# Linear half of six groups of up tiles per layer by Strassen's scheme for three of four k pairs; gating on GpSimd, scaled tokens from the third group on

## The chip, the core and the metric

The kernel runs on one core of a Trainium2 chip. Its engines are TensorE (PE in the profile; PEld is its weight load), VectorE (DVE), ScalarE (ACT), GpSimd (POOL) and SyncE (SP), which issues most DMAs. The metric is device time in microseconds (us) of one execution, taken as the median of several runs.

## The reference

A trunk of two layers over 512 tokens of width 1024, in fp32. Each layer mixes tokens (differential attention in layer 0, chunked gated linear attention in layer 1, cross-attention into a memory in both), projects the result, and then runs a gated MLP with a causal depthwise convolution of width 3. The change lies in that MLP alone:

```python
def rms_norm(x, g):
    return x * lax.rsqrt(jnp.mean(x * x, axis=-1, keepdims=True) + EPS) * g

def conv_ffn(h, w_up, conv_w, conv_b, w_down):
    u = h @ w_up                                   # (512, 1024) @ (1024, 5632)
    c = causal_depthwise_conv3(u, conv_w) + conv_b
    a, g = jnp.split(c, 2, axis=-1)                # linear half, gate half: 2816 each
    return (jax.nn.silu(g) * a) @ w_down           # (512, 2816) @ (2816, 1024)

for i in range(2):
    ...
    h = rms_norm(x, ffn_norm[i])
    x = x + conv_ffn(h, w_up[i], conv_w[i], conv_b[i], w_down[i])
```

## The kernel before

Everything is kept transposed: a tile has 128 features on the partitions and the 512 tokens along the free axis. An fp32 product is made of three fp32r products: both operands are split into a high part (a cast, on ACT) and a low part (the difference, on DVE), and the terms high·high, high·low and low·high are summed in PSUM. `product` (L387 to L389) issues these three for each k tile of 128.

**Weights** come in an order fixed by a plan of pieces, packed by the host into blocks of up to 1024 columns. A block is loaded raw by SP (three buffers), and `split_weights` makes `whi` (ACT, L255) and `wlo` (DVE, L258) of it; there are six buffers of each (`WB`). A k tile of an up piece has 256 columns, so a block holds four k tiles and a piece two blocks.

**The feed-forward** of a layer (`ffn`) runs 11 groups, numbered 0 to 10, in three parts (`HALVES` = 4, 4, 3). A group has two output tiles of the linear half (piece `ua`) and two of the gate half (piece `ug`), taken in turn: linear 0, gate 0, linear 1, gate 1. Each output tile has one PSUM bank and eight k tiles, 24 matmuls of 512 columns. The eight banks have the tags mm, sm, lg and tp, two of each, and go round in the order `TURNS`. The operands are the tokens' high and low halves `xsh`, `xsl` as they are before the norm's row scale; `row_scales` computes that scale, rB, during group 0, and each output tile is multiplied by it afterwards. Behind a tile's last matmul follow, in `conv`: the product with rB (DVE, in place in PSUM, L1165), the last tap with scale and bias (ACT, L1167) and the other two taps (DVE, L1168 and L1169). A gate tile then gets silu (ACT, L1333), the gating product with its linear tile is done on DVE (L1334), and the result, `mid`, is split into high (ACT, L1190) and low (DVE, L1191). The results of convolutions rotate through six buffers, `cvo`.

**A down stage** follows each part and multiplies its `mid` tiles by `w_down`. Two k tiles of one piece form a 2x2 block problem (two k tiles by two output tiles, tokens in a left and a right half of 256), which is done by Strassen's scheme in Winograd's form: seven products of 256 columns in place of eight (`seven`, L1247), with sums of weights, sums of operands and a decode of sums at the end. Sums of operands are made in `combine` (L1198 to L1201, four operations of 256 columns into a tile `tsum`, on POOL, or on DVE for the last group of a part); sums of weights in `combined` (L287 to L290, four operations on POOL into one of two tiles `wsum`), which are then split like other weights (ACT L291 and L294, DVE L292 and L295). The decode is L1258 to L1266. Four pieces in the last part of layer 0 and one in that of layer 1 are done whole, by eight products.

The order of instructions on each engine is the program's own order as written, adjusted by the scheduler of the framework; `order` rows below show it. An engine works its list in order, so an instruction that waits holds back all behind it.

Of the kernel before, what the change touches and what calls it, by code (L numbers as in the profile page):

```python
# [32 lines left out]
WB = 6  # L33
# [52 lines left out]
def _pieces():  # L86
# [6 lines left out]
    for l in range(2):  # L93
# [45 lines left out]

TURNS = ('mm', 'mm', 'sm', 'sm', 'lg', 'lg', 'tp', 'tp')  # L140
# [42 lines left out]
def trunk(ctx, tc, head_d, x_t, mem_t, wpack, cols_a_d, cols_d, conv_d, gate_d, rel_bias, diff_lambda, consts, onehot, out):  # L183
# [94 lines left out]
    def combined(raw, n):  # L278
# [4 lines left out]
        r, wsum = full(raw), sum_pool[0].tile([128, WTILE], F32, name="wsum", bufs=2)  # L283
        a12, a22, a11, a21 = (r[:, :, i] for i in range(4))
        sv = wsum[:, :512 * pairs].rearrange("p (i j c) -> p i j c", i=4, j=pairs)
        s1, s2, s3, s4 = (sv[:, i] for i in range(4))
        ADD.tensor_add(s1, a21, a22)  # L287
        ADD.tensor_sub(s3, a11, a21)
        ADD.tensor_sub(s2, s1, a11)
        ADD.tensor_sub(s4, a12, s2)  # L290
# [3 lines left out]
        A.copy(h1[:, m], wsum[:, m])  # L294
        V.tensor_sub(l1[:, m], wsum[:, m], h1[:, m].bitcast(F32))  # L295
        out = []
        for j in range(pairs):
            own = lambda t, i: t[:, 512 * j + 128 * i:512 * j + 128 * i + 128]
            new = lambda t, i: t[:, 128 * (pairs * i + j):128 * (pairs * i + j) + 128]
# [3 lines left out]
        return out  # L303

    def make_block(raws=None):
# [9 lines left out]
        if plan[i][0][0] == "dn":  # L315
            made[i] += combined(raw, n)
# [8 lines left out]
    ADD = G  # L325


    def weights(key, by_block=False):
# [3 lines left out]
        if i + 1 < len(plan) and plan[i + 1][0][0] in ("dn", "dw"):  # L332
            limit = first_of[i + 1] + 1
# [814 lines left out]
    def ffn(pool, l, acc):  # L1148
        rB = pool.tile([128, S], F32, name="rB", bufs=1)
        sum_pool[0] = pool  # L1150
        old = list(zip(xh, xl))
        nu = [0]
# [4 lines left out]
        def up(parts, n, ops):  # L1157
            i = nu[0]
            nu[0] += 1
            p = bank(TURNS[i % 8])  # L1160
            product(p, parts, n, ops)
            return p

        def conv(p, j):
            V.tensor_mul(p, p, rB)  # L1165
# [27 lines left out]
        left, right = blk(0, 256), blk(1, 256)  # L1193

        def combine(b2, b1, bh, bl, fh, fl, E):
            t = pool.tile([128, 2 * S], F32, name="tsum", bufs=1)
# [15 lines left out]
        def down(base, nq, mids, pairs, tags, last, acc2):  # L1212
# [88 lines left out]
            if whole[3]:  # L1301
                start(3)
                while done[0] < first_of[first + 4]:
                    make_block()
# [139 lines left out]
```

## Time and profile before

| | |
|---|---|
| median of 3 runs | 1149.63 us (1149.5 to 1149.68) |
| the profiled execution, its own time | 1150.36 us |
| its span, first to last instruction | 1148.5 us |
| feed-forward of layer 0 | some 240 to 594 us of the span; its down stages at 328 to 368 and 456 to 496 |
| feed-forward of layer 1 | some 792 to 1136 us; its down stages at 880 to 920, 1007 to 1048 and 1113 to 1136 |

A row of a group gives the line, the engine, the operation with output and input tile (partitions x elements and type), the number of instructions, and after the bar the total busy time, the mean duration of one in ns, and the idle time of the engine just before them with what ended it. A row of a timeline gives the start, the duration, the engine and the instruction, and in brackets how long the engine waited for what before it. A row of windows gives a stretch of the span, its length, the busy time of each engine with its count of instructions, the granted TensorE clock (1.00 is full speed), the DMA share and GB/s. A matmul's record overlaps with the next one's, so the pace is read from a window, not from the duration of one.

### The profile page before, as it was taken

The page shows a single profiled execution, that of the slowest core. Times are in us where ns is not written, and L with a number is a line of the kernel's source. Part 1 is how long each engine was busy: PE and PEld are TensorE (multiplying, and loading weights), DVE is VectorE, ACT ScalarE, POOL GpSimd, SP SyncE. Part 2 cuts the span into 40 slices and gives each one's busy share as a digit, 9 for nine tenths or more (in the row PEclk, how much of TensorE's full clock was granted, in tenths as well). Part 3 has the DMA queues.
Part 4 walks back from the last instruction along what each step waited for, and adds up shares of the span by engine and source line. Part 5 has one row for each costly group of instructions (what it writes and reads, how often), then busy time and mean ns, then how long its engine had stood idle before and what let it go on. Part 6 is the DMA issues. An engine that isn't in the chain of part 4 may idle for free.

```text
span 1148.5 us, 16655 instructions
## 1 busy us (share of the span) xinstructions
PE 1142.7 (99%) x6311; PEld 985.1 (86%) x6311; DVE 871.2 (76%) x1455; ACT 592.0 (52%) x1032; POOL 193.2 (17%) x230
## 2 busy tenths in 40 slices
PE   9999999999999999999999999999999999999998
PEld 7888888888899888988888888988888988899887
DVE  8576778688789677977677637777887977797777
ACT  6676686555454354434457634535644444453442
POOL 0000000001543125500000000000135403360340
PEclk9999999999999999999999999999999999999999
DMA  9522242133214322343252220333241342234212
GB/s 293 173 83 84 78 142 74 58 109 110 92 57 146 111 77 80 96 144 100 69 182 70 100 94 12 101 125 119 74 126 40 127 149 74 61 91 143 92 46 102
DMA packets 39662, 117.83 MB, mean 103 GB/s; under 512 B 4767, under 2 KB 7256, under 8 KB 39582
## 3 DMA queue, kind: packets, MB, share of 16 engines
q1 hardware_dynamic: 39150, 116.37, 31.8%
q8 instruction: 50, 0.82, 0.3%
q10 hardware_dynamic: 432, 0.39, 0.1%
q14 instruction: 30, 0.25, 0.1%
HBM read 112.54 MB, written 4.21 MB: 102 GB/s over the span
## 4 chain that ended last, share of the span: by engine, by line
PE 99%; DMA 0%; DVE 0%; ACT 0%; issue 0%
PE ps_mm L365 6%; PE ps_mm L367 6%; PE ps_mm L366 6%; PE ps_mm L387 6%; PE ps_mm L388 6%; PE ps_mm L389 6%; PE ps_lg L1247 5%; PE ps_sm L388 5%; PE ps_sm L389 5%; PE ps_sm L387 5%; PE ps_mm L1247 4%; PE ps_tp L388 4%; PE ps_lg L388 4%; PE ps_tp L387 4%; PE ps_lg L387 4%; PE ps_tp L389 4%
## 5 line engine op out<-in xcount | busy, mean ns | idle before, releaser
L258 DVE TENSOR_TENSOR wlo<-raw,whi 128x1024 fp32r<-128x1024 f32 (+4 forms) x174 | 194.2, 1127 | 77.0 <-ACT whi L255 76.4
L255 ACT CAST whi<-raw 128x1024 fp32r<-128x1024 f32 (+4 forms) x174 | 168.0, 976 | 124.2 <-PE ps_sm L388 29.8
L365 PE MATMUL ps_mm<-whi,xsh 128*128 128x512 f32 (+2 forms) x328 | 126.2, 385 | 0.0
L367 PE MATMUL ps_mm<-whi,xsl 128*128 128x512 f32 (+2 forms) x328 | 123.0, 375 | 0.0
L366 PE MATMUL ps_mm<-wlo,xsh 128*128 128x512 f32 (+2 forms) x328 | 122.8, 374 | 0.0
L387 PE MATMUL ps_mm<-xsh,whi 128*128 128x512 f32 x278 | 109.3, 393 | 0.0
L388 PE MATMUL ps_mm<-xsl,whi 128*128 128x512 f32 x278 | 108.4, 390 | 0.0
L389 PE MATMUL ps_mm<-xsh,wlo 128*128 128x512 f32 x278 | 108.2, 389 | 0.0
L387 PE MATMUL ps_sm<-xsh,whi 128*128 128x512 f32 x218 | 84.8, 389 | 0.0
L388 PE MATMUL ps_sm<-xsl,whi 128*128 128x512 f32 x218 | 84.8, 389 | 0.0
L389 PE MATMUL ps_sm<-xsh,wlo 128*128 128x512 f32 x218 | 84.8, 389 | 0.0
L365 PEld LDWEIGHTS ps_mm<-whi,xsh 128*128 128x128 f32 x328 | 61.7, 188 | 11.4 <-issue 1.0
L367 PEld LDWEIGHTS ps_mm<-whi,xsl 128*128 128x128 f32 x328 | 61.7, 188 | 11.3
L366 PEld LDWEIGHTS ps_mm<-wlo,xsh 128*128 128x128 f32 x328 | 61.8, 188 | 10.1
L387 PE MATMUL ps_lg<-xsh,whi 128*128 128x512 f32 x160 | 62.2, 389 | 0.0
L388 PE MATMUL ps_lg<-xsl,whi 128*128 128x512 f32 x160 | 62.2, 389 | 0.0
L389 PE MATMUL ps_lg<-xsh,wlo 128*128 128x512 f32 x160 | 62.2, 389 | 0.0
L387 PE MATMUL ps_tp<-xsh,whi 128*128 128x512 f32 x160 | 62.2, 389 | 0.0
L388 PE MATMUL ps_tp<-xsl,whi 128*128 128x512 f32 x160 | 62.2, 389 | 0.0
L389 PE MATMUL ps_tp<-xsh,wlo 128*128 128x512 f32 x160 | 62.2, 389 | 0.0
L389 PEld LDWEIGHTS ps_mm<-xsh,wlo 128*128 128x128 f32 x278 | 52.2, 188 | 11.0
L387 PEld LDWEIGHTS ps_mm<-xsh,whi 128*128 128x128 f32 x278 | 52.2, 188 | 10.8 <-issue 0.3
(382 smaller groups left out, 2835.4 us busy)
## 6 DMA issues: line engine op xcount, KB each, us to landing
raw<-in_wpack_dram SPq DMA_DIRECT2D x178, 512.0 KB, 3.5
xt<-in_x_t_dram SPq DMA_DIRECT2D x15, 256.0 KB, 5.2
raw<-in_wpack_dram SPq DMA_DIRECT2D x15, 256.0 KB, 3.1
raw<-in_wpack_dram SPq DMA_DIRECT2D x8, 384.0 KB, 3.0
xres<-xt SPq DMA_DIRECT2D x8, 256.0 KB, 3.2
xt<-xres SPq DMA_DIRECT2D x8, 256.0 KB, 5.8
out_dram<-xt SPq DMA_DIRECT2D x7, 256.0 KB, 2.0
bt<-bias_d SPq DMA_DIRECT2D x6, 256.0 KB, 4.1
```

Of the source, the lines that this page charges most:

```text
L255: ins = A.copy(hi[:, c], raw[:, c])
L258: V.tensor_sub(lo[:, c], raw[:, c], hi[:, c].bitcast(F32))
L365: mm(p, sh[k][:, blk(b)], hi, start=k == 0, stop=False)
L366: mm(p, sh[k][:, blk(b)], lo, start=False, stop=False)
L367: mm(p, sl[k][:, blk(b)], hi, start=False, stop=k == KT - 1)
L387: mm(p, hi[:, blk(n)], bh, start=i == first, stop=False)
L388: mm(p, hi[:, blk(n)], bl, start=False, stop=False)
L389: mm(p, lo[:, blk(n)], bh, start=False, stop=i == last)
L1247: mm(banks[c][b][:, h], w, v, start=b not in seen[c], stop=m == nq - 1 and t == 2 and i in close)
```

## The change

Six groups of each layer, 4 to 9 (`SEVEN`), compute the linear half by seven products where they can. The piece `ua` of such a group takes its k tiles in the order (6,7), (4,5), (0,1), (2,3). The pair (6,7) is done by eight products as before; the other three pairs by seven products of 256 columns, summed over the pairs in four banks and decoded once (`up_by_seven`). So both linear tiles of such a group come before its gate tiles. `combined` gets a count of plain pairs: the first block of a piece keeps one pair plain and makes sums for one pair, the second makes sums for two.

The scheme needs sums of tokens in which a row scale cannot be taken out behind, since the decode adds up products. From group 2 on (`SCALED`) the operands are therefore tokens already multiplied by rB: `scaled` multiplies on POOL (L1294), scales by the norm's gain on ACT (L1295), and `scaled_token` splits them (L1265, L1266): tokens 0 to 2 behind the second tile pair of group 0, 3 to 5 behind the first of group 1, 6 and 7 behind the second of group 1. `conv` leaves the rB product out from group 2 on. `token_sums` scales two tokens again and makes their sums on POOL, once a layer: for (4,5) behind the second tile pair of group 2, for (0,1) and (2,3) behind the two of group 3.

The gating product goes to POOL (L1428), but for the last group of each part, where it stays on DVE. Sums of weights, of `mid` tiles and of tokens now share the two tiles `wsum`; `mid2` has 8 buffers instead of 9. Weight blocks are made by one `refill` in up and down stages, within the six buffers, and banks come from a running counter over `TURNS`. The bytes and the number of loads stay as they were.

```diff
-                piece(("ua", l, q), "w_up", l, K8, (256 * q, 256 * q + 256))
+                ks = (6, 7, 4, 5, 0, 1, 2, 3) if q in SEVEN else K8
+                piece(("ua", l, q), "w_up", l, ks, (256 * q, 256 * q + 256))
...
+SCALED = 2
+SEVEN = (4, 5, 6, 7, 8, 9)
...
-    def combined(raw, n):
+    def combined(raw, n, plain):
...
-        r, wsum = full(raw), sum_pool[0].tile([128, WTILE], F32, name="wsum", bufs=2)
-        a12, a22, a11, a21 = (r[:, :, i] for i in range(4))
+        r, wsum, js = full(raw), sum_tile(), pairs - plain
+        a12, a22, a11, a21 = (r[:, plain:, i] for i in range(4))
...
-        A.copy(full(h0)[:, :, :3], r[:, :, :3])
-        V.tensor_sub(full(l0)[:, :, :3], r[:, :, :3], full(h0)[:, :, :3].bitcast(F32))
-        m = slice(0, 512 * pairs)
+        if plain:
+            c = slice(0, 512 * plain + 384)
+            split_weights(c, raw, h0, l0)
+        else:
+            A.copy(full(h0)[:, :, :3], r[:, :, :3])
+            V.tensor_sub(full(l0)[:, :, :3], r[:, :, :3], full(h0)[:, :, :3].bitcast(F32))
+        m = slice(0, 512 * js)
...
+    def sum_tile():
+        return sum_pool[0].tile([128, WTILE], F32, name="wsum", bufs=2)
...
+        def take(n):
+            nb[0] += n
+            return [bank(TURNS[i % 8]) for i in range(nb[0] - n, nb[0])]
+
+        def refill():
+            nonlocal live
+            while done[0] < min(len(order), first_of[min(used[0] + 2, len(plan))]) and live + sizes[done[0]] <= WB:
+                live += sizes[done[0]]
+                make_block()
...
+        def up_by_seven(i):
+            b, seen = take(4), set()
+            where = [(2, left), (0, left), (0, right), (1, left), (3, right), (2, right), (3, left)]
+            for m, ks in enumerate(((6, 7), (4, 5), (0, 1), (2, 3))):
+                while len(made) <= i or len(made[i]) <= m:
+                    refill()
+                part = made[i][m]
+                if m == 0:
+                    for n in range(2):
+                        product(b[n], part, n, [tokens[k] for k in ks], range(2), 99)
+                else:
+                    for r in steps:
+                        c, h = where[r]
+                        (hi, lo), (vh, vl) = part[r], sums_of[ks][r]
+                        for t, (w, v) in enumerate(((hi, vh), (hi, vl), (lo, vh))):
+                            mm(b[c][:, h], w, v, start=c > 1 and c not in seen, stop=m == 3 and t == 2 and r in (2, 5, 6, 3))
+                            seen.add(c)
+                if m % 2:
+                    release(i, 2, m == 3)
+            u, w = ctile(), ctile()
+            A.copy(u[:, left], b[2][:, left])
+            V.tensor_add(w[:, right], u[:, left], b[2][:, right])
+            V.tensor_add(u[:, right], w[:, right], b[3][:, right])
+            V.tensor_add(w[:, left], w[:, right], b[3][:, left])
+            V.tensor_add(w[:, right], u[:, right], b[3][:, left])
+            V.tensor_add(b[0], b[0], u)
+            V.tensor_add(b[1], b[1], w)
+            return b[:2]
 
-        def conv(p, j):
-            V.tensor_mul(p, p, rB)
+        def conv(p, j, scaled):
+            if not scaled:
+                V.tensor_mul(p, p, rB)
...
-            t = pool.tile([128, 2 * S], F32, name="tsum", bufs=1)
+            t = sum_tile()
...
+        def scaled(k):
+            t = ctile()
+            G.tensor_mul(t, xT[k], rB)
+            A.activation(t, t, AF.Copy, scale=c_ffn(l, k))
+            return t
+
+        def scaled_token(k):
+            t = scaled(k)
+            if k < 6:
+                y = pool.tile([128, 2 * S], F32R, name="hsc", bufs=6)
+                hi, lo = y[:, :S], y[:, S:]
+            else:
+                hi, lo = split_tiles()
+            parts_of(t, hi, lo)
+            return hi, lo
+
+        def token_sums(ks):
+            (bh, bl), (fh, fl) = (tokens[k] for k in ks)
+            tiles = [split_tiles() for _ in range(2)]
...
+            combine(scaled(ks[0]), scaled(ks[1]), None, None, None, None, G, parts)
...
+                if q == SCALED:
+                    tokens = fresh
+                a, c2, ops, ca = begin(("ua", l, q)), [], [], None
+                if q in SEVEN:
+                    ca = [conv(p, 2 * q + n, True) for n, p in enumerate(up_by_seven(a))]
...
-                    V.tensor_mul(ca, ca, cg)
-                    c2.append(ca)
+                    end = q == base + nq - 1
+                    (V if end else G).tensor_mul(cn, cn, cg)
+                    c2.append(cn)
...
+                    if 0 < 2 * q + n < 4:
+                        fresh += [scaled_token(k) for k in range(len(fresh), min(len(fresh) + 3, KT))]
+                    if SEVEN and 4 < 2 * q + n < 8:
+                        token_sums(((4, 5), (0, 1), (2, 3))[2 * q + n - 5])
```

In the rows below `[waits ...]` names the engines and DMA queues whose earlier work an instruction waits for. The first place is ACT at the end of group 1 in layer 0, where `cvo`, `mid` and `xsh` are the tiles of that name above. Before:

```order
L255 CAST whi<-raw 128x1024 [waits DMAHW0_49,PE_49]
L1190 CAST mid<-cvo 128x512 [waits DVE_49]
L1167 ACTIVATE cvo<-ps_tp,cv_81 128x512 [waits DVE_49]
L255 CAST whi<-raw 128x1024 [waits DMAHW1_49,PE_49]
L255 CAST whi<-raw 128x1024 [waits DMAHW2_49,PE_49]
L1167 ACTIVATE cvo<-ps_tp,cv_81 128x512 [waits DVE_49]
L1333 ACTIVATE cvo<-cvo 128x512 [waits DVE_49,Activation_49]
L1190 CAST mid<-cvo 128x256 [waits DVE_49]
L1190 CAST mid_3002<-tsum 128x1024 [waits Pool_49]
```

The same place now:

```order
L1242 ACTIVATE cvo<-ps_tp,cv_81 128x512 [waits DVE_49]
L258 CAST whi<-raw 128x1024 [waits DMAHW1_49,PE_49]
L1242 ACTIVATE cvo<-ps_tp,cv_81 128x512 [waits DVE_49]
L1295 ACTIVATE cvo<-cvo,cols 128x512 [waits Pool_49] x2
L258 CAST whi<-raw 128x1024 [waits DMAHW2_49,PE_49]
L1426 ACTIVATE cvo<-cvo 128x512 [waits DVE_49,Activation_49]
L1265 CAST mid<-cvo 128x256 [waits Pool_49]
L1265 CAST xsh<-cvo 128x512 [waits Activation_49] x2
L1265 CAST mid_3059<-wsum 128x1024 [waits Pool_49]
```

Two scalings of tokens (6 and 7) have come between the convolution (L1242, before L1167) and silu (L1426, before L1333), and the casts of these two tokens stand behind the cast of `mid`, which now waits for POOL's gating.

The second place is POOL where the sums of weights for the first down stage of layer 0 are made. Before, sums of `mid` tiles and of weights stand beside each other:

```order
L1198 TENSOR_TENSOR tsum<-cvo 128x256 [waits DVE_49]
L1200 TENSOR_TENSOR tsum<-cvo 128x256
L1199 TENSOR_TENSOR tsum<-cvo,tsum 128x256 [waits Pool_49]
L1201 TENSOR_TENSOR tsum<-cvo,tsum 128x256 [waits Pool_49]
L287 TENSOR_TENSOR wsum<-raw 128x256 [waits DMAHW0_49,DVE_49]
L288 TENSOR_TENSOR wsum<-raw 128x256
L289 TENSOR_TENSOR wsum<-wsum,raw 128x256 [waits Pool_49]
L290 TENSOR_TENSOR wsum<-raw,wsum 128x256 [waits Pool_49]
```

Now the token scalings and token sums stand between the sums of weights (L290 to L293 are before's L287 to L290):

```order
L290 TENSOR_TENSOR wsum<-raw 128x256 [waits DMAHW7_49,DVE_49]
L291 TENSOR_TENSOR wsum<-raw 128x256
L292 TENSOR_TENSOR wsum<-wsum,raw 128x256 [waits Pool_49]
L293 TENSOR_TENSOR wsum<-raw,wsum 128x256 [waits Pool_49]
L1294 TENSOR_TENSOR cvo<-xt,rB 128x512 x2
L1271 TENSOR_TENSOR wsum<-cvo 128x256 [waits DVE_49,Activation_49]
L1273 TENSOR_TENSOR wsum<-cvo 128x256
L1272 TENSOR_TENSOR wsum<-cvo,wsum 128x256 [waits Pool_49]
L1274 TENSOR_TENSOR wsum<-cvo,wsum 128x256 [waits Pool_49]
L290 TENSOR_TENSOR wsum<-raw 128x256 [waits DMAHW0_49,DVE_49]
L291 TENSOR_TENSOR wsum<-raw 128x256
L292 TENSOR_TENSOR wsum<-wsum,raw 128x256 [waits Pool_49]
```

The sums of tokens go into `wsum`, wait for ACT's scaling, and the next block's sums stand behind them in the list.

The third place is ACT at the border between the groups 6 and 7 of layer 0, ahead of the second down stage; this is the list as it is now, whose L1229 is the copy that opens the decode of a linear half:

```order
L1265 CAST mid<-cvo 128x512 [waits Pool_49]
L258 CAST whi<-raw 128x1024 [waits DMAHW4_49,PE_49]
L1242 ACTIVATE cvo<-ps_mm,cv_81 128x512 [waits PE_49]
L1426 ACTIVATE cvo<-cvo 128x512 [waits DVE_49,Activation_49]
L298 CAST whi<-raw 128x2x384 [waits DMAHW5_49,PE_49]
L1265 CAST mid<-cvo 128x256 [waits Pool_49]
L1265 CAST mid_4616<-wsum 128x1024 [waits Pool_49]
L301 CAST whi<-wsum 128x1024 [waits PE_49,Pool_49]
L1229 COPY cvo<-ps_lg 128x256 [waits PE_49]
L298 CAST whi<-raw 128x2x384 [waits DMAHW6_49,PE_49]
L301 CAST whi<-wsum 128x1024 [waits PE_49,Pool_49]
```

The decode's copy stands behind the cast of `mid` and the cast of its sums, both of which wait for POOL, and behind a cast of sums of weights.

More of the change, by code (lines that the diff above doesn't have):

```diff
@@ L1235, in release, with emitted, seven @@
-            def release(c, m):
-                nonlocal live
-                piece = first + c
+            def start(c):
+                begin(("dw" if whole[c] else "dn", l, base, c))
+                banks[c] = take(2 if whole[c] else 4)
+            def emitted(c, m):
                 if m == nq - 1 or m % 2:
-                    live -= 1 if whole[c] else 2
+                    release(first + c, 1 if whole[c] else 2, m == nq - 1)
+            def seven(c, m, some=steps):
+                while len(made) <= first + c or len(made[first + c]) <= m:
@@ L1240, in release @@
                     refill()
-            def seven(c, m, some=steps):
                 for i in some:
@@ L1354, in ffn @@
                     load(gw[32 * b:32 * b + 17], gate_d)
-            down(base, nq, mids, pairs, nu[0] // 4 % 2, last, acc2)
+            down(base, nq, mids, pairs, last, acc2)
             base += nq
```

148 lines of the change are left out of this document (79 added, 69 removed).

## The prediction

> **What bounds the kernel now.** Groups are numbered 0 to 10 as in the program; down stages follow groups 3, 7 and 10. I read the page first: busy shares, then the chain that ended last.
>
> ```profile
> PE 1142.7 (99%) x6311; PEld 985.1 (86%) x6311; DVE 871.2 (76%) x1455; ACT 592.0 (52%) x1032; POOL 193.2 (17%) x230
> PE 99%; DMA 0%; DVE 0%; ACT 0%; issue 0%
> ```
>
> TensorE is the whole chain; nothing else ever ends a wait. So an edit gains what it takes from PE's stream, and loses whenever another engine becomes late for PE. For the price of a matmul I took windows of PE alone, one inside an up stage (512 columns), one inside a down stage (256 columns, already by seven products):
>
> ```profile
> core 0: us, PE busy (x), PEclk, DMA share, GB/s
> 260.00:320.00 60.00, 60.00 (x266) 1.00 0.29 94
> 330.00:366.00 36.00, 36.00 (x303) 1.00 0.35 111
> ```
>
> Without the two or three that only reach over an edge: 60/264 = 0.227 us for 512 columns, 36/300 = 0.120 us for 256. The half width costs 0.53 of the full one. Next, how much room the other engines have, from windows of all engines: the first two groups of the feed-forward, then the first two down stages of layer 0.
>
> ```profile
> core 0: us, PE busy (x) PEld busy (x) DVE busy (x) ACT busy (x) POOL busy (x), PEclk, DMA share, GB/s
> 255.90:289.30 33.40, 33.40 (x149) 27.67 (x148) 29.69 (x39) 18.51 (x23) 3.06 (x4) 1.00 0.35 111
> 328.00:368.00 40.00, 40.00 (x334) 39.96 (x333) 37.91 (x52) 19.07 (x25) 22.10 (x20) 1.00 0.36 110
> 456.00:496.00 40.00, 40.00 (x335) 40.00 (x334) 37.23 (x50) 18.56 (x25) 18.25 (x19) 1.00 0.36 115
> ```
>
> DVE's average of 76% hides that it is 89 to 95% busy exactly here. PE has no wait in these stretches, but no reserve behind it.
>
> **The gain.** One pair of k tiles costs 12 matmuls of 512 (2.73 us) by eight products, 21 of 256 (2.52 us) by seven: 0.21 us less. Six groups, three pairs, two layers are 36 pairs: **7.4 us**, and that is all that PE can gain. If the cover of the rest holds, the run ends at 1150.4 - 7.4 = 1143.0 (the profiled execution took 1150.36; the median of the runs is 0.7 less).
>
> **The work around it**, from groups of instructions with shapes apart:
>
> ```profile
> L290 POOL TENSOR_TENSOR wsum<-raw,wsum 128x256 f32<-128x256 f32 x35 | 42.7, 1221 | 2.7
> L289 POOL TENSOR_TENSOR wsum<-wsum,raw 128x256 f32<-128x256 f32 x35 | 37.4, 1068 | 0.0
> L288 POOL TENSOR_TENSOR wsum<-raw 128x256 f32<-128x256 f32 x35 | 30.9, 882 | 0.0
> L1201 POOL TENSOR_TENSOR tsum<-cvo,tsum 128x256 f32<-128x256 f32 x14 | 10.3, 737 | 0.7
> L288 POOL TENSOR_TENSOR wsum<-raw 128x128 f32<-128x128 f32 x3 | 1.4, 462 | 0.0
> L258 DVE TENSOR_TENSOR wlo<-raw,whi 128x1024 fp32r<-128x1024 f32 x143 | 172.7, 1219 | 70.7 <-ACT whi L255 70.2
> L295 DVE TENSOR_TENSOR wlo<-wsum,whi 128x1024 fp32r<-128x1024 f32 x35 | 47.9, 1368 | 1.5 <-ACT whi L294 1.3
> L1334 DVE TENSOR_TENSOR cvo<-cvo 128x512 f32<-128x512 f32 x44 | 33.3, 757 | 15.9 <-ACT cvo L1333 15.9
> L1165 DVE TENSOR_TENSOR ps_sm<-ps_sm,rB 128x512 f32<-128x512 f32 x24 | 16.6, 693 | 1.4 <-PE ps_sm L389 1.3
> L1191 DVE TENSOR_TENSOR mid<-cvo,mid 128x512 fp32r<-128x512 f32 x28 | 19.7, 704 | 2.4 <-ACT mid L1190 2.1
> L1261 DVE TENSOR_TENSOR cvo<-cvo,ps_lg 128x256 f32<-128x256 f32 x10 | 4.2, 421 | 0.8
> L294 ACT CAST whi<-wsum 128x1024 fp32r<-128x1024 f32 x35 | 36.7, 1049 | 25.3 <-POOL wsum L290 14.5 <-PE ps_sm L388 7.3 <-PE ps_tp L388 3.5
> L1190 ACT CAST mid<-cvo 128x512 fp32r<-128x512 f32 x28 | 17.3, 619 | 8.8 <-DVE cvo L1334 8.0
> L345 ACT ACTIVATE xsh<-xt,cols 128x512 fp32r<-128x512 f32 x16 | 11.5, 716 | 3.9 <-DVE xt L1111 3.9
> ```
>
> DVE loses 72 scalings by rB (x 0.693 = 50 us) and 32 gatings (x 0.757 = 24). It gains twelve decodes of four 256-column and two 512-column sums (4 x 0.421 + 2 x 0.69 = 3.1, 37 us), the low halves of 1152 more weight columns a piece (sums included: 3200 where there were 2048; 12 x 1.37 x 1152/1024 = 18), 16 scaled tokens and 12 halves of token sums (28 x 0.704 = 20). 74 against 75: even. POOL gains 180 instructions: 96 weight sums, 24 token sums, 32 gatings and 28 token scalings. The last 60 have 512 columns, which the trace does not show on POOL: 256 against 128 columns differ by 0.275 (0.737 - 0.462, the quickest rows), so 0.737 + 2 x 0.275 = 1.29 us alone.
>
> POOL's price depends on DVE. In the timeline:
>
> ```profile
> 331.18 1.21 DVE L295 TENSOR_TENSOR wlo<-wsum,whi 128x1024 fp32r<-128x1024 f32 x1
> 331.33 1.66 POOL L290 TENSOR_TENSOR wsum<-raw,wsum 128x256 f32<-128x256 f32 x1
> 333.08 0.75 DVE L1169 SCALAR_TENSOR_TENSOR cvo<-ps_tp,cv,cvo 128x510 f32<-128x510 f32 x1
> 333.66 0.73 POOL L288 TENSOR_TENSOR wsum<-raw 128x256 f32<-128x256 f32 x1
> ```
>
> Under a DVE subtraction with both inputs in SBUF, 256 columns take 1.66 us; beside one that reads PSUM, 0.73. The four weight sums average about 1.01. So 512 columns in company: 1.29 x 1.01/0.737 = 1.77.
>
> [...]
>
> **Place A, start of group 2.** It is the first to use scaled tokens, and PE reaches tokens 6 and 7 with its 19th product. Timeline of before at that border (PE starts group 2 at 284.67):
>
> ```profile
> 284.67 0.39 PE L387 MATMUL ps_mm<-xsh,whi 128*128 128x512 f32 x1
> 288.75 0.39 PE L387 MATMUL ps_mm<-xsh,whi 128*128 128x512 f32 x1
> 286.79 0.78 ACT L1167 ACTIVATE cvo<-ps_tp,cv 128x512 f32<-128x512 f32 x1 [1.09 <-DVE ps_tp L1165]
> 289.41 0.63 ACT L1333 ACTIVATE cvo<-cvo 128x512 f32<-128x512 f32 x1 [1.85 <-DVE cvo L1169]
> 290.07 0.69 DVE L1334 TENSOR_TENSOR cvo<-cvo 128x512 f32<-128x512 f32 x1 [0.76 <-ACT cvo L1333]
> 290.80 0.41 ACT L1190 CAST mid<-cvo 128x256 fp32r<-128x256 f32 x1 [0.76 <-DVE cvo L1334]
> ```
>
> ACT's new order puts the casts of tokens 6 and 7 behind that last cast, which waits for POOL's gating, which waits for silu. Before, the cast ends at 291.21. Now two scalings (2 x 0.716) and a weight cast (1.05) stand between convolution and silu, 0.6 beyond the 1.85 it waited anyway; gating takes 1.29 for 0.69, 0.6 more; token 6's cast adds 0.62: 293.0 against 288.75, and its low half (0.70 against a matmul's 0.23) 0.5 more: 4.7 us. DVE was 29.69 of 33.40 busy ahead of it; six low halves (4.2) less three gatings (2.3), and POOL in company, make it about 3.5 later, and gating in company 0.5. **8.7 us; layer 1 has one weight cast more before the convolution, 9.7.** Bounds 4.7 and 12 each.
>
> **Place B, first down stage.** From the end of group 2 to the last weight sum of this stage POOL's list holds 44 operations of 256 columns and five of 512, where before it held 24. It cannot begin before silu, 5.4 us in, that is 16.4 before the stage. In company: 44 x 1.01 + 5 x 1.77 = 53.3, done at +36.9. That block is needed at +35.3 (fourth piece, third product group: 14 x 2.52), less cast and low half (1.05 + 1.37): +32.9. 4.0 late, if POOL never waits. It does: token sums wait for ACT's scaling, and weight sums now share two buffers with token and end-group sums that DVE must first read (ACT and DVE each twice round, about 4 x 2 us). DVE, 37.91 of 40 full, cannot catch up. **12 us per layer**; alone (0.737, 1.29) POOL is done at +22.5 and only the buffer wait is left, 2.5; at 1.22 per operation 20.
>
> **Place C, groups 4 to 7 and the second down stage.** After a group's last matmul (0): weight cast 1.05 and convolution to 2.0, DVE's low half and two steps to 3.9, silu 4.5, gating 6.3, cast 6.7, five POOL operations 11.8, cast 12.8; three narrow sums meanwhile, cast and copy to 14.2. But the next linear half is done at 10.3, so its decode is 3.9 late; with it and two weight halves 19.7, convolutions 23.0. The gate half's first tile, its silu, gating and casts follow in order, and the next last convolution starts at 28.6, where 22.5 would be on time: **6.1 us lag per group** (3.5 by the prices alone). After two borders 12.2; the down stage takes the banks of group 7's linear half 21.9 after the border, while its convolutions end at 23 + 12.2 + 1.5 = 36.7: 14.8 (7.2 alone), part of it perhaps already at group 7's own banks. The stage's late last sums add 2: **17 us per layer**. The third stage in layer 1 has only two such groups and a plain one behind: 2 in all.
>
> **Sum:** 18.4 + 24 + 34 + 2 - 7.4 = +71; 1150.4 + 71 - 0.7 = **1221 us**. DMAs, attention and the tail keep their counts: nothing.
>
> **Rivals.** (1) *The saving arrives*, PE never waits: 1142. For it: DVE's total is even and every engine's average has room. It decides if POOL's sums and gating run so early that no list holds PE's operands back; the lists above put them behind silu. (2) *Only latency, no contention*: POOL at 0.74 and 1.29. A 14, B 5, C 18: 1150.4 + 37 - 7.4 = 1180. For it: DVE's PSUM operations do not disturb POOL. Against: weight sums average 1.01. [...] (4) *The change does little*: if SEVEN had no pieces PE would count the same; its list shows 324 matmuls more, so I give it nothing.
>
> **How the numbers follow.** Forecast (1195 to 1236) 0.50, rival 2 (1155 to 1195: its places may come out shorter still, but A's lower bound, 2 x 4.7, alone outweighs the gain) 0.23, rival 3 (1236 to 1262) 0.17, rival 1 0.07, lands within 0.2% by accident 0.03 (0.2%, 2.3 us, is what runs of this kernel can tell apart). Range 1166 to 1253: it leaves out rival 1, the accident and the ends of 2 and 3, 0.2 in all. Faster 0.07, same 0.03, slower 0.90.
>
> **What would show it.** PE waits of 5 to 10 us at token 6's product in group 2; waits for whi and wlo in the first down stage, ACT there waiting for POOL's wsum; a wait of 7 us or more at the second down stage's first products for DVE; POOL near 400 us busy, 512 columns above 1.5. Wrong if PE stays 99% without waits, or if these places wait under 2 us each.

## The result, and the profile after

The changed kernel takes **1250.3 us** (median of 4 runs, 1249.86 to 1251.1) against 1149.66 (median of 4): the ratio is 1.0873, with a 95% interval of 1.0854 to 1.0892. The forecast was 1221, range 1166 to 1253.

The page of the changed kernel: its busy shares, and the granted clock in 40 slices.

```profile
span 1249.3 us, 17749 instructions
PE 1168.8 (94%) x6635; PEld 1017.8 (81%) x6635; DVE 908.0 (73%) x1475; ACT 639.8 (51%) x1124; POOL 405.6 (32%) x410
PEclk9999999997989998899999999999799899889999
```

Two sums follow from it and from the page before. PE now stands idle for 1249.3 - 1168.8 = 80.5 us, where it was 1148.5 - 1142.7 = 5.8: **74.7 us more waiting**. And PE is busy for 26.1 us longer although it has 7.4 us less to do: **33.5 us in which it is busy but slow**. 74.7 + 33.5 - 7.4 = 100.8, which is the whole difference of the spans. The digits below 9 in the clock row say where a part of the second sum lies.

What PE waits for, summed over both layers (time, number, longest):

```profile
PE ps_mm L398 <- ACT xsh L1265: 21.0, 2, 11.8
PE ps_sm L1342 <- DVE cvo L1244: 15.2, 2, 7.7
PE ps_lg L1224 <- DVE cvo L1244: 12.4, 2, 6.2
PE ps_lg L1342 <- ACT whi L301: 10.8, 4, 2.7
PE ps_sm L1342 <- DVE mid L1266: 4.5, 5, 1.7
...
```

The smaller rows are left out here, but counted in the sums that follow. The waits fall into three kinds, which the text below calls by the prediction's letters. **A**: products of an up stage that wait for scaled tokens (L398 to L400), 23.7 us. **B**: products of a down stage (L1342 here) that wait for weights or `mid` tiles, 25.1, the third stage included. **C**: products that wait for a PSUM bank, that is for a convolution that still reads it (here its last step, L1244), 27.6.

Place A in layer 0, from the timeline (start, duration):

```profile
293.19 0.78 ACT L1242 ACTIVATE cvo<-ps_tp,cv 128x512 f32<-128x512 f32 x1 [2.83 <-DVE ps_tp L1240]
...
293.87 1.32 ACT L1295 ACTIVATE cvo<-cvo,cols 128x512 f32<-128x512 f32 x2
...
296.47 0.63 ACT L1426 ACTIVATE cvo<-cvo 128x512 f32<-128x512 f32 x1 [0.35 <-DVE cvo L1244]
...
298.66 0.41 ACT L1265 CAST mid<-cvo 128x256 fp32r<-128x256 f32 x1 [1.56 <-POOL cvo L1428]
...
298.97 1.14 ACT L1265 CAST xsh<-cvo 128x512 fp32r<-128x512 f32 x2
...
299.64 0.79 PE L398 MATMUL ps_mm<-xsh,whi 128*128 128x512 f32 x1 [9.24 <-ACT xsh L1265]
...
302.36 0.63 PE L399 MATMUL ps_mm<-xsl,whi 128*128 128x512 f32 x1
...
302.79 0.63 PE L400 MATMUL ps_mm<-xsh,wlo 128*128 128x512 f32 x1
```

This is the list of ACT that the prediction read: silu at 296.47, then the cast of `mid`, which waits 1.56 us for POOL's gating, and only behind it the cast of token 6, which PE has waited 9.24 us for. The last two rows show what comes after: two matmuls of 512 columns start 0.43 us apart, where 0.227 was the pace before. The granted clock of such stretches, in windows of PE (from, to, length, PE busy, records, clock):

```profile
299.70:306.10 6.40, 5.92 (x14) 0.52 0.13 53
...
472.40:480.00 7.60, 7.60 (x48) 0.73 0.26 71
...
501.10:508.00 6.90, 6.90 (x35) 0.56 0.25 76
```

All three stand right behind a wait of 6 us or more, at A and twice at C.

The lag at C is read from the copy that opens each decode (the timeline's ACT rows):

```profile
408.42 0.37 ACT L1229 COPY cvo<-ps_sm 128x256 f32<-128x256 f32 x1 [2.14 <-PE ps_sm L1224]
...
433.55 0.37 ACT L1229 COPY cvo<-ps_mm 128x256 f32<-128x256 f32 x1
...
459.45 1.05 ACT L1265 CAST mid<-wsum 128x1024 fp32r<-128x1024 f32 x1 [3.82 <-POOL wsum L1274]
460.83 0.62 ACT L301 CAST whi<-wsum 128x512 fp32r<-128x512 f32 x1 [0.33 <-POOL wsum L293]
461.36 0.37 ACT L1229 COPY cvo<-ps_tp 128x256 f32<-128x256 f32 x1
```

In group 4 ACT waits for PE, and the copy is in time. The next copies come 25.1 and 27.8 us later, though PE does such a group in 21.2:

```profile
410.00:431.20 21.20, 21.20 (x125) 1.00 0.25 77
```

So each group adds 4 to 7 us of lag, and what stands ahead of the copy at 461.36 is a cast that waited 3.82 us for POOL's sums of `mid`. The same window shows the gain: 123 products and two that reach over an edge in 21.2 us, against 96 x 0.2275 = 21.84 before, 0.64 a group where 0.63 was forecast. **The saving of 7.4 us is there; it is only buried.**

### The profile page after: what moved, and what is told of

It is laid out like the page before. It is cut to its first block, busy times and chain, and to the rows that moved or that the text cites. A ratio compares the mean times of both kernels' runs of the same rounds, so it can differ in the third digit from the quotient of the medians.

```text
span 1249.3 us, 17749 instructions
## 1 busy us (share of the span) xinstructions
PE 1168.8 (94%) x6635; PEld 1017.8 (81%) x6635; DVE 908.0 (73%) x1475; ACT 639.8 (51%) x1124; POOL 405.6 (32%) x410
## 4 chain that ended last, share of the span: by engine, by line
PE 67%; POOL 14%; DVE 12%; ACT 6%; issue 2%; ACTq 0%; POOLq 0%; DVEq 0%
PE ps_mm L376 6%; PE ps_mm L378 6%; PE ps_mm L377 6%; PE ps_mm L399 3%; PE ps_mm L400 3%; PE ps_mm L398 3%; PE ps_lg L1342 3%; PE ps_mm L1342 3%; POOL cvo L1428 3%; PE ps_tp L1342 3%; PE ps_tp L225 2%; PE ps_sm L398 2%; PE ps_sm L399 2%; PE ps_sm L400 2%; PE ps_sm L1342 2%
## 5 line engine op out<-in xcount | busy, mean ns | idle before, releaser
L261 DVE TENSOR_TENSOR wlo<-raw,whi 128x1024 fp32r<-128x1024 f32 (+5 forms) x162 | 188.1, 1172 | 86.4 <-ACT whi L258 84.1
L258 ACT CAST whi<-raw 128x1024 fp32r<-128x1024 f32 (+5 forms) x162 | 153.9, 962 | 89.0 <-PE ps_mm L399 16.0
L1428 POOL TENSOR_TENSOR cvo<-cvo 128x512 f32<-128x512 f32 x32 | 45.9, 1433 | 251.7 <-ACT cvo L1426 251.7
L301 ACT CAST whi<-wsum 128x1024 fp32r<-128x1024 f32 (+1 forms) x62 | 58.6, 946 | 121.0 <-POOL wsum L293 121.0
L302 DVE TENSOR_TENSOR wlo<-wsum,whi 128x1024 fp32r<-128x1024 f32 (+1 forms) x62 | 77.4, 1249 | 52.4 <-ACT whi L301 52.4
L290 POOL TENSOR_TENSOR wsum<-raw 128x256 f32<-128x256 f32 (+1 forms) x62 | 60.0, 967 | 81.6 <-DVE wlo L302 38.1
L398 PE MATMUL ps_mm<-xsh,whi 128*128 128x512 f32 x150 | 60.8, 405 | 21.0 <-ACT xsh L1265 21.0
L1342 PE MATMUL ps_lg<-mid,whi 128*128 128x256 f32 x280 | 57.9, 297 | 12.2 <-ACT whi L301 10.8
L1266 DVE TENSOR_TENSOR mid<-cvo,mid 128x512 fp32r<-128x512 f32 (+1 forms) x44 | 37.0, 842 | 42.3 <-ACT mid L1265 42.3
L1342 PE MATMUL ps_sm<-mid,whi 128*128 128x256 f32 x228 | 48.6, 298 | 19.7 <-DVE cvo L1244 15.2
L293 POOL TENSOR_TENSOR wsum<-raw,wsum 128x256 f32<-128x256 f32 (+1 forms) x62 | 62.6, 1010 | 4.6
L1342 PE MATMUL ps_mm<-mid,whi 128*128 128x256 f32 x304 | 61.5, 293 | 0.8 <-ACT whi L301 0.8
L292 POOL TENSOR_TENSOR wsum<-wsum,raw 128x256 f32<-128x256 f32 (+1 forms) x62 | 61.3, 989 | 0.0
L400 PE MATMUL ps_mm<-xsh,wlo 128*128 128x512 f32 x150 | 59.4, 396 | 0.0
```

Source lines behind the costliest of these rows:

```text
L258: ins = A.copy(hi[:, c], raw[:, c])
L261: V.tensor_sub(lo[:, c], raw[:, c], hi[:, c].bitcast(F32))
L293: G.tensor_sub(s4, a12, s2)
L398: mm(p, hi[:, blk(n)], bh, start=i == first, stop=False)
L400: mm(p, lo[:, blk(n)], bh, start=False, stop=i == last)
L1342: mm(banks[c][b][:, h], w, v, start=b not in seen[c], stop=m == nq - 1 and t == 2 and i in close)
```

## The experiments

Each run is the changed kernel with an edit; experiments 10 and 12 are medians of four executions, the others one execution each. The letters A, B and C below are PE's waits of the three kinds, summed from the view of waits; in the changed kernel they are 23.7, 25.1 and 27.6.

### 1. Gating on DVE

```diff
-(V if end else G).tensor_mul(cn, cn, cg)
+V.tensor_mul(cn, cn, cg)
```

> The change with every gating product on DVE again. Theory L (the order of ACT's list holds PE's operands back, and gating on POOL is one link of 1.45 us against 0.70 of chains of 10 us and more): each chain gets some 0.75 to 1.5 us shorter per gating, two gatings per group, so about 10 to 15 us come back: 1235 to 1241. Rival P (POOL's gating itself is what PE waits for): the waits at the start of group 2 and at the second down stage go, some 31 + 38 us: about 1181. Rival D (DVE has no room for 24 us more): slower than 1250.

**1223.26 us**, A 16.5, B 20.3, C 17.3. Twice as much came back as theory L said, but no kind of wait went: neither theory's number. Gating on POOL accounts for some 27 us, as a link in all three chains, and not only by the 0.7 us by which one gating is longer (1.43 us on average against 0.76 before). At A it had another effect that L left out: POOL's gating also slowed DVE, to 1.37 us from 0.69 for one subtraction (last section).

### 2. No group by seven products

```diff
-SEVEN = (4, 5, 6, 7, 8, 9)
+SEVEN = ()
```

> The change with no group by seven products (no token sums, no weight sums in up stages), scaled tokens and gating on POOL kept. Theory L: the wait at the start of group 2 stays whole (14.1 + 16.6 us with the slow stretch behind it), the waits at the first and second down stage go, and so does the 7.4 us of saved products: 1150.4 + 30.7 = 1181, 1175 to 1190. Rival P: gating on POOL alone delays the sums of weights of the first down stage, which keeps its 32 us: about 1213. Rival F (all losses come from the seven products): 1150.

**1179.6 us**, as L said (1181). All that is left of the waits, in the view of waits:

```profile
PE ps_mm L398 <- ACT xsh L1265: 21.0, 2, 11.8
PE ps_mm L399 <- DVE hsc L1266: 1.8, 2, 1.0
PE ps_mm L399 <- DVE xsl L1266: 1.0, 2, 0.5
```

A is whole, to a tenth of a microsecond, and B and C are gone. So A needs none of the seven products: it belongs to the scaled tokens with gating on POOL, and experiment 1 shows that 16.5 of it stay when gating is on DVE. B and C need the seven products with their sums; gating on POOL and scaled tokens by themselves make no down stage late.

### 3. Scaled tokens earlier

```diff
-if 0 < 2 * q + n < 4:
-    fresh += [scaled_token(k) for k in range(len(fresh), min(len(fresh) + 3, KT))]
+if 0 < 2 * q + n < 3:
+    fresh += [scaled_token(k) for k in range(len(fresh), min(len(fresh) + 4, KT))]
```

> The change with the scaled tokens made as four and four behind the second tile pair of group 0 and the first of group 1, so that tokens 6 and 7 no longer stand behind the last gating of group 1. Theory L: the wait at the start of group 2 goes in both layers, with its slow clock, 30.7 us: 1219, no PE wait over 2 us between 280 and 310. Rival D (DVE, near full there, is the reason, and works the same total): at most half comes back, 1235 or more, with PE waits of 4 us or more for DVE at that place.

**1236.55 us**, A 9.3 with a longest wait of 4.8. The time is rival D's, the waits are not: what stays at A is 8.0 us for ACT's casts of scaled tokens and 1.3 for DVE, where D asked for waits of 4 us for DVE. Taking the two tokens out from behind the last gating brings back 14 of 24 us. That the rest stays because the same work now has to be done sooner is likely, but no run shows it.

### 4. Sums of mid tiles behind the next decode

```diff
-ca = [conv(p, 2 * q + n, True) for n, p in enumerate(up_by_seven(a))]
+banks = up_by_seven(a)
+while late:
+    mids.append(late.pop()())
+ca = [conv(p, 2 * q + n, True) for n, p in enumerate(banks)]
...
-mids.append(mid_sums(c2, ops, V if end else G))
+sums = lambda c2=c2, ops=ops, E=V if end else G: mid_sums(c2, ops, E)
+if not end and q + 1 in SEVEN:
+    late.append(sums)
+else:
+    mids.append(sums())
```

> The change with the sums of mid tiles of groups 4, 5, 6 and 8 written behind the decode of the next group's linear half instead of ahead of it. Theory L (the decode stands on ACT and DVE behind a cast that waits for POOL's four sums): the lag per group falls from some 6 to 1 or 2 us, the waits at group 7 and the second down stage go in both layers, 38 us with their slow clock, or at least two thirds of it: 1212 to 1225. Rival W (the lag comes from the work added to DVE and POOL, which stays the same): within 5 us of 1250.

**1236.04 us**, C 14.7, half of what it was, between what L and W said. But the edit moved less than it was written for: the order of the trace is not that of the text. At groups 5 and 6 the cast of the sums still stands ahead of the decode's copy on ACT, in both layers, and the copies come as late as in the change (433.30 and 460.86, against 433.55 and 461.36). This is group 5 of layer 0:

```profile
432.34 1.05 ACT L1265 CAST mid<-wsum 128x1024 fp32r<-128x1024 f32 x1 [4.05 <-POOL wsum L1274]
433.30 0.36 ACT L1229 COPY cvo<-ps_mm 128x256 f32<-128x256 f32 x1
```

Only at group 7 does the cast come behind the copy, which starts at 481.33 where it was 491.44. So the half of C that went goes with the order at this one border. What else holds the copy back there can be seen ahead of it:

```profile
474.88 0.63 ACT L1429 ACTIVATE cvo<-cvo 128x512 f32<-128x512 f32 x1 [1.89 <-DVE cvo L1244]
...
478.05 0.74 POOL L293 TENSOR_TENSOR wsum<-raw,wsum 128x256 f32<-128x256 f32 x1
...
478.74 1.29 POOL L1431 TENSOR_TENSOR cvo<-cvo 128x512 f32<-128x512 f32 x1
...
480.06 0.41 ACT L1265 CAST mid<-cvo 128x256 fp32r<-128x256 f32 x1 [3.84 <-POOL cvo L1431]
...
481.33 0.36 ACT L1229 COPY cvo<-ps_lg 128x256 f32<-128x256 f32 x1
```

Silu is done at 475.5, but gating starts at 478.74, since POOL has four sums of weights ahead of it; the cast and the copy wait behind.

### 5. Both: gating on DVE, sums later

> The first and the fourth experiment together: gating on DVE, and the sums of mid tiles written behind the next decode. Losses at the places as those runs showed them: group 2 some 21 us (both layers), first down stage 31, and at group 7 and the second and third down stages 28 with either edit alone or more. Theory L (the rest there is the cast of mid behind POOL's gating, which in the fourth experiment stood behind sums of weights): these 28 fall to 6 or less: 1143 + 21 + 31 + 6 = 1201, 1195 to 1205. Rival D (the gatings take the room on DVE that the deferred sums need): they stay above 20: 1215 or more.

**1211.96 us**, A 16.5, B 19.4, C 10.4: between what L and D said. The two edits add up only in part (C is 17.3 and 14.7 with one of them). The run does not test L, though, because the sums did not come later: in the trace their cast stands ahead of the copy at groups 5, 6 and 7 alike. At group 7 of layer 0:

```profile
474.88 1.05 ACT L1265 CAST mid<-wsum 128x1024 fp32r<-128x1024 f32 x1 [5.63 <-POOL wsum L1274]
...
477.52 0.36 ACT L1229 COPY cvo<-ps_lg 128x256 f32<-128x256 f32 x1
```

So the 10 us of C that are left still have the wait for POOL's sums of `mid` ahead of them, and what C would be without both links no run shows. The same order stands in the traces of experiments 8 and 10, which carry this edit too.

### 6. Token sums off POOL, and earlier

```diff
-            combine(scaled(ks[0]), scaled(ks[1]), None, None, None, None, G, parts)
+            combine(rescaled(ks[0]), rescaled(ks[1]), None, None, None, None, G, parts)
...
+        def rescaled(k):
+            t = ctile()
+            V.scalar_tensor_tensor(t, xT[k], c_ffn(l, k), rB, op0=ALU.mult, op1=ALU.mult)
+            return t
...
-if SEVEN and 4 < 2 * q + n < 8:
-    token_sums(((4, 5), (0, 1), (2, 3))[2 * q + n - 5])
+if SEVEN and 3 < 2 * q + n < 7:
+    token_sums(((4, 5), (0, 1), (2, 3))[2 * q + n - 4])
```

> The change with the tokens for the token sums scaled by one DVE operation each in place of one on POOL and one on ACT, and the token sums one tile pair earlier. Theory L (in the first down stage POOL's list is too long): POOL loses six operations of 1.75 us there and has four sums earlier, about 15 us less to do in the stage: the waits of 32 us with their slow clock go to under 8: 1218 to 1228. Rival S (the two shared sum buffers, with ACT and DVE in between, hold POOL back): at most half goes: 1234 or more. Group 2 and the later places stay as in the change.

**1239.91 us**, A 23.7, B 16.8, C 30.6. A third of B went, and C grew by 3. The time is on rival S's side (at most half goes), but experiment 9 speaks against S's cause. What holds B after this edit is not decided by this run.

### 7. Scaled tokens from group 3 on

```diff
-SCALED = 2
+SCALED = 3
...
-if 0 < 2 * q + n < 4:
-    fresh += [scaled_token(k) for k in range(len(fresh), min(len(fresh) + 3, KT))]
+if 2 * q + n < 5:
+    fresh += [scaled_token(k) for k in range(len(fresh), len(fresh) + (0, 2, 2, 2, 2)[2 * q + n])]
```

> The change with scaled tokens from group 3 on instead of group 2, two tokens made behind each of four tile pairs; 4 more products with rB on DVE per layer, the rest as it is. Theory L (tokens 6 and 7 stand at the end of a list that ends in silu, gating and casts): now they have a whole group of 16 us to be ready, the wait goes in both layers: 1250 - 31 = 1219, 1217 to 1225. Rival D (DVE cannot make the tokens in time because it is full in groups 0 to 2): PE waits over 3 us at group 3 or earlier, 1232 or more.

**1244.18 us**, rival D's time: A falls to 8.0, its longest wait being 3.0, and B rises to 33.1. PE waits less in one place, and the lists of ACT, DVE and POOL, as late as before, meet it in the next.

### 8. All four edits

Experiments 1, 4 and 6 with scaled tokens from group 3 on, made two, three and three behind tile pairs 1, 2 and 3.

> All of it: gating on DVE, mid sums behind the next decode, scaled tokens from group 3 on (two, three and three behind three tile pairs), token sums scaled on DVE and one tile pair earlier. Theory L (each loss has its own place and its own list): 0 to 2 us at group 2 or 3, 0 to 10 in the first down stage, 0 to 6 later, against 7.4 us of products saved: 1143 to 1161. Rival D (the edits move 24 us of gating, 8 of scaling and 6 of rB products onto DVE, which is then full): PE waits for DVE over 30 us in all, 1175 or more.

**1200.79 us**, A 0, B 22.5, C 11.8. L was far too hopeful, and the time is on rival D's side. But DVE is not full: in the stretch with the worst waits its windows (PE, PE loads, DVE, ACT and POOL busy) are

```profile
320.00:340.00 20.00, 16.10 (x76) 14.12 (x75) 14.34 (x17) 7.18 (x11) 13.63 (x14) 0.83 0.07 27
340.00:360.00 20.00, 12.80 (x73) 11.78 (x73) 14.35 (x18) 8.42 (x13) 10.99 (x14) 0.83 0.26 77
```

No engine is busy for more than 14.4 of 20 us beside PE, and PE waits all the same. That points to the handing over, POOL to ACT to DVE to PE, in lists that are worked in order; no run takes it apart.

### 9. Token sums in buffers of their own

```diff
-            t = sum_tile()
+            t = [xtile() for _ in range(2)]
```

> The change with the sums of tokens written into tiles of the token ring instead of the two shared wsum buffers; POOL's work and all else as in the change. The first down stage loses 16 us per layer there. Theory S (the shared buffers make a ring: POOL's next sums wait until ACT and DVE have read the last ones, and those stand behind other waits): at least half of it goes, 1250 - 16 to 1250 - 32 = 1218 to 1234, with POOL's waits for DVE's wlo and xsl gone there. Theory L (POOL's list of operations is too long for the stage): POOL has as much to do as before, 1244 to 1252.

**1250.41 us**, nothing gained; B 22.1, C 30.6. Token sums in the two shared sum buffers are not the cause: a part of the prediction's place B that does not hold. Sums of weights and of the end group still share the two here, which was not tried apart.

### 10. Fewer groups, token sums behind the first down stage

Groups 6, 8 and 9 by seven products, gating on DVE, sums as in 4, scaled tokens as in 8, and token sums at groups 4 and 5. Its token sums are made of x after the first down stage has added to it, by the same number of operations of the same sizes. So they belong to other tokens than the scheme needs, and the run stands for a time only, not for a kernel that computes the trunk.

> Seven products only in groups 6, 8 and 9; scaled tokens from group 3 on (two, three and three behind three tile pairs); token sums in groups 4 and 5, behind the first down stage, scaled on DVE and in tiles of their own; gating on DVE; mid sums behind the next decode. PE saves 6 pieces x 3 pairs x 0.21 = 3.8 us. Theory L (each loss belongs to lists that meet at one place: token sums and weight sums in the first down stage, four groups in a row ahead of the second): no loss at group 2 or 3 as in the eighth run, none in the first down stage as in the second, 0 to 2 us at the second, 0 to 4 at the third in layer 1: 1146 to 1152. Rival D (scaling and gating on DVE in the early groups, or one group by seven products, are enough to make PE wait): 1158 or more.

**1171.93 us**, ratio 1.0188 (1.0171 to 1.0205), A 0, B 14.7, C 0: rival D's side. The waits are many and short (the longest in a down stage 1.3 us). C is nothing here although the sums of `mid` still stand ahead of the copies.

### 11. Groups 6 to 9, all else as in the change

Token sums at groups 4 and 5, of a token's high and low part added up on POOL.

> The change with seven products in groups 6 to 9 only, so that the token sums can come behind the first down stage (groups 4 and 5; x has been added to by then, so POOL adds a token's high and low part in place of scaling x again, and ACT's scaling falls away). Gating, tokens and all else as in the change. PE saves 4 x 3 x 2 pairs x 0.21 = 5.0 us. Theory L: group 2 keeps its 31 us, the first down stage loses nothing (its 32 us came from token sums between its sums of weights), and two groups in place of four ahead of the second down stage bring half the lag or less: of 38 us there 8 to 19 stay, the third keeps 7: 1150.4 - 5.0 + 31 + 0 + 8 to 19 + 7 = 1191 to 1202. Rival P (gating and weight sums on POOL are enough to make the first down stage late): 16 to 32 us more there, 1210 to 1234. Rival K (the second down stage is late by the last group alone, however many go ahead): 38 stay there, 1221.

**1220.56 us**, A 23.8, B 5.1, C 26.7. In the first down stage PE has no wait at all; its window:

```profile
320.00:400.00 80.00, 80.00 (x513) 1.00 0.30 97
```

So B there comes from the token sums, as L said; the up stages' own sums of weights, which fall away with groups 4 and 5, stand behind the stage's in POOL's list. C stays whole with half of the groups, which is rival K's number. But it is no proof that the lag does not add up, for the very first group by seven products is already late here. Its last product and the copy of its decode in the timeline:

```profile
437.13 0.28 PE L1224 MATMUL ps_mm<-xsh,wlo 128*128 128x256 f32 x1
...
444.79 1.05 ACT L1265 CAST mid<-wsum 128x1024 fp32r<-128x1024 f32 x1 [3.83 <-POOL wsum L1274]
...
446.70 0.37 ACT L1229 COPY cvo<-ps_sm 128x256 f32<-128x256 f32 x1
```

The copy comes 9.3 us after the product, behind the same cast as in the change. Whether the lag ahead of it is that of token sums, which now stand in groups 4 and 5, or of gating and `mid` sums on POOL in a group by eight products was not told apart.

### 12. Sums behind the first down stage, gating mixed

Groups 6, 8, 9 in layer 0 and 6 in layer 1; token sums as in 11; scaled tokens as in 8; gating on POOL but for the last group of a part and the second tile of a group by seven. The sums of group 8 that the expectation names are not made in layer 0, so that part of the edit does nothing.

> Seven products in groups 6, 8 and 9 of layer 0 and 6 of layer 1; scaled tokens from group 3 on (two, three and three behind three tile pairs); token sums behind the first down stage as in c1; gating on POOL but for the last group of a part and the second tile of a group by seven products; mid sums of group 8 behind the next decode. PE saves 4 x 3 x 0.21 = 2.5 us. Theory L: group 2 and 3 lose 0 to 4 us, the first down stage 0 to 4, the second 0 to 6 in both layers, the third nothing: 1148 to 1160; below 1149 only if all three are nothing. Rival D (DVE, with the tokens to split in groups 0 and 1, comes late to the first down stage whatever POOL does, 4 to 5 us per layer as in the tenth run, and to the second as well): 1160 to 1172.

**1191.07 us**, ratio 1.0361 (1.0344 to 1.0379), A 0, B 24.5, C 0, and 1.2 us in which an up stage waits for weights: slower than both theories said. It differs from experiment 10 in gating, in who makes the token sums and into which tiles, and in the groups of layer 1. Of the 19 us between them 10 are waits of kind B; which difference costs them stays open.

No run beats the kernel before. Experiments 10 and 2 come nearest; 10 does not compute the trunk, and 2 saves no product at all.

## Why the prediction was right, and where it was not

**The direction and the places** were right. The time, 1250, lies outside the forecast's own band (1195 to 1236), in that of rival 3, and inside the stated range because this reached to 1253. *The gain*: 0.64 us a group measured, 0.63 forecast. *Place A*: forecast 18.4 us, measured 23.7 of waits. The mechanism was the one described, and experiment 2 shows that it needs no seven products. The size was off because silu came at 296.47 and not at 289.41 + 4.1: the convolution ahead of it waited 2.83 us for DVE, which was later than the 3.5 us allowed. *Place C*: forecast 34, measured 27.6; a lag of 6.1 us per group was forecast, 3.9 and 6.6 measured between the first three copies. Experiments 1 and 4 show its two links, gating on POOL and, at group 7, the sums of `mid`. *Place B*: forecast 24 in the first down stages and 2 in the third stage of layer 1, measured 19.9 and 4.3 (and 1.0 in the second ones). Token sums among sums of weights make the first (experiments 2 and 11); that they share the sum buffers does not (9). The sum of the three, 78.4 forecast and 76.4 measured, is closer than its parts, and that is luck: the forecast of A was too small, that of C too large.

**The step that failed** is the sum itself: it priced a wait at its own length. 33.5 us came on top, in which PE was busy but slow, and they make the difference between 1221 and 1250, since the waits themselves came out near their sum. The rows behind the waits show the clock at 0.52 to 0.73. By the trace's clock records PE was busy at half clock for some 52 us, which loses 26 of the 33.5. The other 7 are not the clock: experiment 10, whose clock stays at 1.00, also has PE busy for 8.9 us more than its work (1147.8 against 1142.7, with 3.8 us saved), and it has short waits only. The forecast gave the slow clock no price: behind the wait at place A, at a clock of 0.52, two matmuls start 0.43 us apart (302.36 and 302.79), against 0.227 at 1.00 before. The last section has half clock behind short waits too, where PE was busy for 0.41 and 0.45 of the 3.4 us ahead.

**Rival 3's** band (1236 to 1262) holds the measured time, but not by POOL's price: the highest that place B reckoned with, 1.22 us for 256 columns, is not what the changed kernel's sums of weights take on average. Its groups with shapes apart:

```profile
L290 POOL TENSOR_TENSOR wsum<-raw 128x256 f32<-128x256 f32 x47 | 50.2, 1069 | 47.6 <-DVE wlo L302 31.5 <-DVE mid L1266 9.5 <-DVE xsl L1266 5.7
...
L1294 POOL TENSOR_TENSOR cvo<-xt,rB 128x512 f32<-128x512 f32 x28 | 47.4, 1714 | 0.1
L1428 POOL TENSOR_TENSOR cvo<-cvo 128x512 f32<-128x512 f32 x32 | 45.9, 1433 | 251.7 <-ACT cvo L1426 251.7
```

1.07 and 1.71 are near the forecast's prices (1.01 and 1.77) and 1.43 lies below; the four sums of weights (L290 to L293) average 1.04. The first row's idle time is the wait for a sum buffer; experiment 9 shows that to spare token sums that wait gains nothing. **Rival 1** and **rival 2** fell with the waits.

**Two smaller faults.** DVE was to come out even; it is busy for 36.8 us more (908.0 against 871.2), part of it spent beside POOL. And the window from 255.9 to 289.3, called the first two groups, holds 149 records where a group has 96 products: it is some one and a third groups ahead of group 2 and the first 4.6 us of that. Its busy shares stand.

## What to carry to other kernels

Where one engine is 99% busy, a saving on it is worth no more than the slack of every list that feeds it. Count what a change adds to these lists as links, each with its wait, and not as busy time: here DVE, the next in line, reaches 90% in three of the 40 slices of the changed kernel's page, ACT and POOL in none, and 7.4 us of products saved cost 75 us of waits. Then price the slow stretch of TensorE behind its waits as well, here another 33.5 us. Moving work to an idle engine adds a link wherever the result goes back to the engine it came from.

## What the runs showed of the hardware that was not expected

The clock did not fall at every wait, and the longest wait did not decide it. In the down stages of experiment 10 PE waits 1.3 us at most, several times in a row, and these windows keep the full clock:

```profile
334.00:346.00 12.00, 8.90 (x63) 1.00 0.32 95
465.00:478.00 13.00, 9.22 (x64) 1.00 0.29 85
```

In experiment 12 two waits of 1.0 and 0.9 us within 3.4 us are followed by half clock:

```profile
465.00:468.40 3.40, 1.53 (x10) 1.00 0.48 154
468.40:471.90 3.50, 3.50 (x19) 0.51 0.02 5
```

In the first down stage of the changed kernel, where no wait is over 2.8 us, one such stretch is followed by half clock and the next is not:

```profile
353.70:357.10 3.40, 1.41 (x9) 0.99 0.53 154
357.10:360.50 3.40, 3.40 (x18) 0.51 0.01 2
360.50:363.90 3.40, 1.74 (x14) 1.00 0.00 0
363.90:367.30 3.40, 3.18 (x26) 1.00 0.02 5
```

What separates these rows is the share for which PE was busy: 0.45 and 0.41 are followed by half clock, 0.51, and 0.74 and 0.71 over the longer stretches of experiment 10, are not. The stretches of half clock in the changed kernel's clock records last 3.4 us or a multiple of it, up to 17.1. Right ahead of each of these eleven stretches PE was busy for 0 to 0.48 of 3.4 us (1.64 of 3.42 at most, from 954.38 to 957.80). Of the 3.4 us steps at full clock, counted from the clock's changes, the least busy one with full clock behind it has 0.50 (1.69 of 3.41, from 950.97 to 954.38). No run varies this share by itself.

POOL slowed DVE here as well as DVE POOL. POOL's timeline in the changed kernel, gating and then scaling, and DVE's:

```profile
284.38 1.29 POOL L1428 TENSOR_TENSOR cvo<-cvo 128x512 f32<-128x512 f32 x1 [1.37 <-ACT cvo L1426]
...
287.33 1.74 POOL L1294 TENSOR_TENSOR cvo<-xt,rB 128x512 f32<-128x512 f32 x1
```

```profile
283.80 0.69 DVE L1266 TENSOR_TENSOR hsc<-cvo,hsc 128x512 fp32r<-128x512 f32 x1 [0.20 <-ACT hsc L1265]
284.84 1.37 DVE L1266 TENSOR_TENSOR hsc<-cvo,hsc 128x512 fp32r<-128x512 f32 x1 [0.35 <-ACT hsc L1265]
...
287.85 1.77 DVE L1266 TENSOR_TENSOR hsc<-cvo,hsc 128x512 fp32r<-128x512 f32 x1
```

At 283.80 POOL is idle, and DVE's subtraction takes 0.69 us; beside POOL's gating the same takes 1.37, and beside its scaling 1.77. That scaling takes 1.74, where the one at 281.73 took 1.29 beside steps of DVE that read PSUM. The gating at 284.38, which the change moved to POOL, was thus paid for on DVE as well. These rows stand ahead of place A, where DVE was later than forecast.
